# A second block group in the down projection, the gate's result in its operand's tile, and three smaller edits

## Chip, cores, metric

The kernel runs on one core of a Trainium2 chip. The metric is the device time of one execution in microseconds (us). Five engines work from queues of their own, each in order: PE (TensorE, matrix products), DVE (VectorE), ACT (ScalarE), POOL (GpSimd) and SP (SyncE, which here only issues transfers). An engine that waits at the head of its queue holds up everything queued behind it.

## What is computed

Two layers of a hybrid trunk over T = 1040 positions (16 learned meta tokens and 1024 frames), width 1024. Each layer: norm, one input projection, gated linear attention (GLA) in four heads beside softmax attention with a forget gate (FoX) in eight, an output projection, and a gated feed-forward network with 22 tiles of 128 hidden units.

```python
for i in range(DEPTH):
    xn = rms_norm(h, attn_norm[i])
    gq, gk, gv, gr, glr, fq, fk, fv, ff = jnp.split(xn @ w_in[i], cuts, axis=-1)
    ...
    o_gla = rms_norm(o_gla, ...) * jax.nn.silu(gr)
    ...
    h = h + jnp.concatenate([o_gla, o_fox], axis=-1) @ w_out[i]
    h = h + conv_ffn(rms_norm(h, ffn_norm[i]), w_up[i], conv_w[i], conv_b[i], w_down[i])
return rms_norm(h, final_norm)[:, N_META:]
```

The last step of `conv_ffn` is `(silu(g) * u) @ w_down`: 22 x 128 gated activations times a matrix with 1024 output columns. This is the down projection, where most of the change lies.

## The kernel before

**Products.** Values are kept transposed: 128 features on the partitions, positions along the row. Every fp32 operand is split into a rounded part `hi` (ACT casts) and a remainder `lo` (DVE subtracts), and `mm3` (L221 to L223) makes each product of three matmuls: hi*hi, lo*hi, hi*lo. Layer 0 works on all 1040 positions in two halves of 520 (two pieces of 260 columns each), layer 1 on 1024 in two halves of 512. PE's program is written out by hand; the order on DVE, ACT, POOL and SP is set by a scheduler from the program's dependences. Buffers of one row of T floats come from a shared pool of slots (`s.get`, `s.put`): a slot handed on makes its new writer wait until the old reader is done, be it an engine or a transfer.

**The down projection** (`ffn_down`) adds the products of 19 of the 22 gated tiles to the residual, in groups given by `GROUPS` (L49), each as kind, first tile, number of tiles. The last three tiles (`LAST`) are done by `down_last`, fused with the next layer's norm or with the output.

- "n", tiles 0 to 2: for each of 8 output tiles m, the plain product into PSUM; ACT copies it to a row `do` (L1510), and a transfer on POOL's queue adds the row to the residual `hm` in DRAM (L1512).
- "s", tiles 3 to 10, the block group (`down_blocks`): activations and weights are taken as 2 x 2 blocks (two halves of the hidden tiles; two output tiles, 2j and 2j+1; two halves of the positions), and 7 products of sums of blocks stand for 8. For each pair j the products 1 to 7 are formed in PSUM banks: `a` (two banks taken in turn by j; products 1, 6, 7 and 4 run on into the same sum), `y` for product 2, `x` for 5 and 3. After 1, 6, 7 and 4 ACT copies the sum out into row `du` or `dg` (L1423); after 2, 7 and 3 DVE adds the other bank's content (L1422). Finished rows go to `hm` by an adding transfer (L1437 for 2j+1, L1441 for 2j). The products' order is (0,1) (0,2) (1,1) (0,6) (0,5) (0,7) (0,4) (0,3), then for each later j (j,2) (j,6) (j,5) (j,7) (j+1,1) (j,4) (j,3). Sums of weight blocks are made by DVE (L1038) and split (L1055, L1056), up to four products ahead.
- "r", tiles 11 to 14 and 15 to 18: the residual rows `h0` to `h7` are loaded from `hm` into slots, and DVE adds each plain product to them (L1508).

The operands of later groups are prepared meanwhile (`prepare`, advanced by `pump`): the activations come from DRAM into `st` rows and are split into `ah`, `al` (L335, L336) or into block sums `x1` to `x7`. The weights of `LAST` (`wl`) are split in `down_last`.

**The gate.** `gr_products` (L601 to L631) multiplies a GLA head's output `gog` by silu of the gate, in three column tiles a head: DVE clips the gate into `ge` (L621), ACT takes exp, log and exp (L622 to L624), DVE forms the product in four steps (L625 to L629), the last into `ge` again, and a transfer on POOL's queue carries `ge` to `mixd` (L631). `ge` has one buffer, `gog` two, filled by a load.

**The end.** In the last layer `down_last` goes over three column chunks (512, 384, 128). Each product is added to `h` (L1586), squares are summed for the norm, and `final` scales the rows and stores them (`ot`, L1626). The final of chunk 0 is placed after m = 5 of chunk 1; that of chunk 1 after chunk 2.

**The first norm.** The sums of squares of the input are added on POOL, except those of its second chunk (`j == 1`), which are added on DVE.

## Time and profile before

| | |
|---|---|
| time, median of 3 runs | 2559.34 us (2559.17 to 2566.59) |
| profiled execution: time, span | 2563.32 us, 2561.5 us |
| mean granted TensorE clock | 0.992 |
| busy share of the span: PE, DVE, ACT, POOL | 98%, 69%, 50%, 16% |
| layer 0 down projection: "n", "s", both "r", `down_last` | 34.7, 83.8, 92.0, 34.2 us |
| layer 1: the same | 33.5, 81.2, 88.8, 40.4 us |
| from there to the end | 15.1 us |

The profile gives busy time by engine and by group of instructions, waits by releaser (the instruction or transfer whose end let an engine go on), and a timeline. A wait counted for PE is time in which PE stood; waits on the other engines cost only where PE waits for them later. PE's matmuls overlap: a 260-column one is listed with some 0.28 us, but the next one starts 0.12 us after it.

### The profile page before, as it was taken

The numbers are of one execution on the slowest core, as the hardware profiler recorded it, in microseconds if no ns is written. First come the engines' busy times: TensorE is split into PE (matmuls) and PEld (weight loads), VectorE is DVE, ScalarE is ACT, GpSimd is POOL, SyncE is SP. The second block draws the span as 40 slices with busy tenths as digits, with TensorE's granted clock in tenths as the row PEclk, the third lists the DMA queues.
The fourth block names the chain that finished last, engine by engine and source line by source line (L and its number), as shares of the span: only waits on it lengthen the run. The fifth ranks groups of instructions, "written<-read, shape, count | busy, mean of one in ns | idle before, by whom it ended". The sixth has DMA issues, their size and how long they took to land.

```text
span 2561.5 us, 47017 instructions
## 1 busy us (share of the span) xinstructions
PE 2502.1 (98%) x18430; PEld 2394.3 (93%) x18430; DVE 1776.7 (69%) x3493; ACT 1280.6 (50%) x2737; POOL 420.2 (16%) x587
## 2 busy tenths in 40 slices
PE   8999999999999999999999999999999999999997
PEld 7999999898999999999999899998999999997786
DVE  7656776859877777853666666677697777787545
ACT  6346666635544445641343466665464444455312
POOL 2023334310000000100200334333100000001003
PEclk9999999999999999999999999999999999999998
DMA  3132134342322223763312222143523222257711
GB/s 125 63 94 68 44 94 128 115 140 83 104 84 79 80 83 127 203 159 115 104 57 67 73 79 76 58 143 102 156 78 107 75 81 82 79 167 183 197 54 66
DMA packets 118510, 260.81 MB, mean 102 GB/s; under 512 B 14880, under 2 KB 32544, under 8 KB 118288
## 3 DMA queue, kind: packets, MB, share of 16 engines
q1 hardware_dynamic: 93984, 182.79, 22.9%
q0 software_dynamic: 22432, 72.71, 10.2%
q8 instruction: 144, 2.36, 0.4%
q10 hardware_dynamic: 1872, 2.31, 0.3%
q14 instruction: 78, 0.64, 0.1%
HBM read 177.16 MB, written 67.81 MB: 96 GB/s over the span
## 4 chain that ended last, share of the span: by engine, by line
PE 63%; issue 16%; DVE 12%; ACT 4%; DMA 3%; POOL 1%; SPq 0%; DVEq 0%; POOLq 0%; ACTq 0%
PE mm L221 7%; PE mm L223 7%; PE mm L222 7%; PE up L223 5%; PE up L221 5%; PE up L222 5%; PE down L221 5%; PE down L222 5%; PE down L223 5%; PE av L720 3%; PE tr L694 2%; DVE S L661 2%; ACT P L673 1%; PE S L658 1%; DVE x L1080 1%
## 5 line engine op out<-in xcount | busy, mean ns | idle before, releaser
L221 PE MATMUL up<-x,hi 128*128 128x260 f32 (+1 forms) x2464 | 698.1, 283 | 2.3 <-ACT x L1079 2.1
L223 PE MATMUL up<-x,hi 128*128 128x260 f32 (+1 forms) x2464 | 696.9, 283 | 3.1 <-DVE x L1080 2.9
L222 PE MATMUL up<-x,lo 128*128 128x260 f32 (+1 forms) x2464 | 696.8, 283 | 0.0
L223 PEld LDWEIGHTS up<-x,hi 128*128 128x128 f32 x2464 | 466.2, 189 | 4.6 <-DVE x L1080 4.6
L221 PEld LDWEIGHTS up<-x,hi 128*128 128x128 f32 x2464 | 465.1, 189 | 3.8 <-ACT x L1079 3.3
L222 PEld LDWEIGHTS up<-x,lo 128*128 128x128 f32 x2464 | 465.5, 189 | 0.4 <-DVE lo L1056 0.3
L1056 DVE TENSOR_TENSOR lo<-raw,hi 128x512 fp32r<-128x512 f32 x364 | 247.8, 685 | 176.2 <-ACT hi L1055 176.2
L221 PE MATMUL mm<-xh,hi 128*128 128x348 f32 (+4 forms) x1056 | 364.1, 345 | 0.0
L223 PE MATMUL mm<-xl,hi 128*128 128x348 f32 (+4 forms) x1056 | 340.0, 322 | 0.0
L222 PE MATMUL mm<-xh,lo 128*128 128x348 f32 (+4 forms) x1056 | 339.3, 321 | 0.0
L1055 ACT CAST hi<-raw 128x512 fp32r<-128x512 f32 x364 | 224.7, 620 | 136.9 <-PE up L223 91.3
L221 PEld LDWEIGHTS mm<-xh,hi 128*128 128x128 f32 x1056 | 199.9, 189 | 5.9 <-issue 5.3
L222 PEld LDWEIGHTS mm<-xh,lo 128*128 128x128 f32 x1056 | 199.8, 189 | 0.4 <-issue 0.3
L223 PEld LDWEIGHTS mm<-xl,hi 128*128 128x128 f32 x1056 | 198.8, 188 | 0.4 <-issue 0.3
L188 ACT CAST hi<-raw 128x512 fp32r<-128x512 f32 (+2 forms) x176 | 102.3, 582 | 190.4 <-PE down L223 106.6
L222 PE MATMUL down<-ah,lo 128*128 128x260 f32 (+1 forms) x528 | 169.2, 320 | 0.1
L221 PE MATMUL down<-ah,hi 128*128 128x260 f32 (+1 forms) x528 | 168.6, 319 | 0.0
L223 PE MATMUL down<-al,hi 128*128 128x260 f32 (+1 forms) x528 | 168.4, 319 | 0.0
L673 ACT ACTIVATE P<-S,m 116x460 f32<-116x460 f32 (+2 forms) x224 | 124.9, 561 | 78.4 <-DVE m L661 74.8
L336 DVE TENSOR_TENSOR PT<-tr,PT 116x464 fp32r<-116x464 f32 (+3 forms) x240 | 123.2, 515 | 48.0 <-ACT PT L335 46.1
L1268 POOL DMA_DIRECT2D actd<-cv x44 | 23.6, 536 | 761.0 <-DVE cv L1267 740.1
L1038 DVE TENSOR_TENSOR raw<-raw,raw 128x512 f32<-128x512 f32 x198 | 129.4, 683 | 15.4 <-DMA raw<-in_wd_dram 13.4
(286 smaller groups left out, 5680.9 us busy)
## 6 DMA issues: line engine op xcount, KB each, us to landing
raw<-in_wm_dram SPq DMA_DIRECT2D x330, 256.0 KB, 2.7
raw<-in_wd_dram SPq DMA_DIRECT2D x64, 256.0 KB, 3.6
actd<-cv POOLq DMA_DIRECT2D x22, 520.0 KB, 3.0
actd<-cv POOLq DMA_DIRECT2D x22, 512.0 KB, 3.2
cb<-cd SPq DMA_DIRECT2D x16, 520.0 KB, 3.8
st<-actd SPq DMA_DIRECT2D x14, 520.0 KB, 5.1
st<-actd SPq DMA_DIRECT2D x14, 512.0 KB, 4.8
kA<-kA SPq DMA_DIRECT2D x24, 260.0 KB, 4.3
```

The costliest lines, as they stand in the source:

```text
L188: nc.scalar.copy(hi[:, :n, :], raw[:, :n, :])
L221: nc.tensor.matmul(ps, wh, xh[:, c0:c0 + n], start=first, stop=False, skip_group_check=more)
L222: nc.tensor.matmul(ps, wl, xh[:, c0:c0 + n], start=False, stop=False, skip_group_check=more)
L223: nc.tensor.matmul(ps, wh, xl[:, c0:c0 + n], start=False, stop=last, skip_group_check=more)
L336: nc.vector.tensor_tensor(out=lo, in0=src, in1=hi.bitcast(F32), op=ALU.subtract)
L661: nc.vector.tensor_tensor_reduce(out=S[:rows, :n], in0=S[:rows, :n], in1=cb[:rows, c0:k1], scale=1.0, scalar=(BIG if ci == 0 else m[:rows, ...
L673: nc.scalar.activation(P[:rows, :n], S[:rows, :n], AF.Exp, scale=-1.0, bias=m[:rows, nch - 1:nch], accum_out=(den if nch == 1 else d3[:row ...
L694: nc.tensor.transpose(tr[:w, 3 - j, :rows], P[:rows, o:o + w], id_)
L720: nc.tensor.matmul(av[:, a:b], w.rearrange("p a b -> p (a b)"), x, start=(t == ts[0] and part == 0 and i == 0), stop=(t == last and i == 1))
L1038: nc.vector.tensor_tensor(out=q[out][:, :nk, :], in0=q[a][:, :nk, :], in1=q[b][:, :nk, :], op=op)
L1055: nc.scalar.copy(hi[:, :nk, :], src[:, :nk, :])
L1056: nc.vector.tensor_tensor(out=lo[:, :nk, :], in0=src[:, :nk, :], in1=hi[:, :nk, :].bitcast(F32), op=ALU.subtract)
```

## The change

1. `GROUPS` becomes n(0,3), s(3,8), n(11,4), s(15,4). Tiles 11 to 14 go through ACT copies and adding transfers, tiles 15 to 18 through a second block group with two hidden tiles in each half (the first has four), so that each of its 28 products is half as long. The residual is loaded late: `h7` and `h6` when product (2,7) of that group is issued, the others as slots come free. For its last pair (output tiles 6 and 7) DVE adds the finished row to `h6`, `h7` in place of the transfer.
2. The weights of `LAST`: the first two tiles are prepared during the second block group.
3. The gate's last step writes into `gog` instead of `ge`, and the transfer to `mixd` reads `gog`.
4. The first norm's second chunk: POOL adds the squares of even k, DVE those of odd k.
5. The end: the final of chunk 0 is placed after m = 3 of chunk 1, and that of chunk 1 is held until the last product has been added to `h`.

```diff
-GROUPS, LAST = (("n", 0, 3), ("s", 3, 8), ("r", 11, 4), ("r", 15, 4)), (19, 3)
+GROUPS, LAST = (("n", 0, 3), ("s", 3, 8), ("n", 11, 4), ("s", 15, 4)), (19, 3)
...
-            to = e if dst is None else dst[:, c0:c0 + n]
+            to = og if dst is None else dst[:, c0:c0 + n]
...
-                nc.gpsimd.dma_start(self.mixd[h][:, c0:c0 + n], e)
+                nc.gpsimd.dma_start(self.mixd[h][:, c0:c0 + n], og)
...
+        def out(j, m, t):
+            if residual and j == NP - 1:
+                h = residual(m)[:, o0:T]
+                nc.vector.tensor_tensor(out=h, in0=t[:, o0:T], in1=h, op=ALU.add)
+            else:
+                nc.gpsimd.dma_start(self.hm[m][:, o0:T], t[:, o0:T], accum_op=ALU.add)
+            s.put(t)
...
+                if residual and (j, p) == (NP - 2, 7):
+                    residual(KD - 1), residual(KD - 2)
...
+        def residual(k):
+            if hT[k] is None:
+                hT[k] = s.get(F32, f"h{k}", first=ids)
                 nc.sync.dma_start(hT[k][:, o0:T], self.hm[k][:, o0:T])
+            return hT[k]
...
-                    blocks = self.down_blocks(lyr, *nxt, X[nxt[0]], pp, fw, halves,
-                                              lambda t=then: len(ahead) < 2 and fetch(t))
+                    more = (lambda t=then: len(ahead) < 2 and fetch(t)) if then else \
+                        (lambda: len(self.last_w[0]) < 2 and self.last_weight(lyr, ids))
+                    blocks = self.down_blocks(lyr, *nxt, X[nxt[0]], pp, fw, halves, more, None if then else residual)
...
-            if not hT:
-                load_residual()
+            for k in range(KD):
+                residual(k)
...
-                elif m == 5 and c0 != dchunks[0][0]:
+                elif m == (5 if c0 + n == T else 3) and c0 != dchunks[0][0]:
                     self.norm_scale(nxt, pp, *before)
...
-                self.final(nxt, hT, pp, *before, pool=KD + 1)
+                with self.tc.issue_after(summed.ins):
+                    self.final(nxt, hT, pp, *before, pool=KD + 1)
...
-                    "square": lambda j: [self.norm_square(nm, *part(j, k), nc.vector if j == 1 else None) for k in range(KD)],
+                    "square": lambda j: [self.norm_square(nm, *part(j, k), nc.vector if j == 1 and k % 2 else None) for k in range(KD)],
```

Line numbers below are those of the changed kernel where its rows are shown: L336 and L337 are the casts and remainders of activations (L335, L336 before), L1056 and L1057 those of weight blocks, L1039 the sums of weight blocks, L1522 and L1524 the "n" copies and their transfers, L1432 and L1433 the block group's adds and copies.

**DVE in the gate, layer 0, at 441 to 445 us of the profile before.** `S`, `m` are a FoX head's scores and row maxima, `PT` its transposed probabilities, `fa`, `fv`, `fy`, `fd` small values of its norm, `gx` the gate's value. Before:

```order
L743 TENSOR_REDUCE fv<-fon 112x2
L625 TENSOR_TENSOR gog<-gx,gog 128x348
L744 TENSOR_TENSOR fv<-fv,fd 112x2
L661 ISA S,m<-S,cb 116x460
L661 ISA m 116x1
L278 SCALAR_TENSOR_TENSOR fa<-fy 112x2
L741 SCALAR_TENSOR_TENSOR fd<-den 116x4
L621 TENSOR_SCALAR ge<-gx 128x348
L279 TENSOR_TENSOR fa<-fa,fv 112x2
L661 ISA S,m<-S,cb,m 116x348
```

Now:

```order
L744 TENSOR_REDUCE fv<-fon 112x2
L622 TENSOR_SCALAR ge<-gx 128x348
L745 TENSOR_TENSOR fv<-fv,fd 112x2
L626 TENSOR_TENSOR gog<-gx,gog 128x348
L662 ISA S,m<-S,cb 116x460
L662 ISA m 116x1
L742 SCALAR_TENSOR_TENSOR fd<-den 116x4
L662 ISA S,m<-S,cb,m 116x348
```

The clip into `ge` has moved ahead of the first of the two score steps; it no longer waits for a transfer that reads `ge`.

**ACT where tiles 11 to 14 end and the second block group begins, layer 0.** Before, the place between the two "r" groups held nothing but weight casts:

```order
L188 CAST hi_14768<-raw_14766 128x512
L188 CAST hi_14826<-raw_14824 128x512
L188 CAST hi_14884<-raw_14882 128x512
L188 CAST hi_14942<-raw_14940 128x512
L188 CAST hi_15000<-raw_14998 128x512
```

Now (`down_14913` and `down_14939` are the two halves of m = 7; `ah_15375` is the last tile's activation, in the slot that row `do_14458` of m = 6 had):

```order
L1056 CAST hi_14901<-raw_14893 128x256
L1522 COPY do_14459<-down_14913 128x520
L336 CAST ah_15375<-st_15179 128x1040
L1522 COPY do_14459<-down_14939 128x520
L1056 CAST hi_14966<-raw2_14905 128x256
L1433 COPY du_14983<-down_14970 128x520
L1056 CAST hi_15004<-raw2_14828 128x256
```

The cast of `ah_15375` stands between the two copies of m = 7. It cannot run before the adding transfer of m = 6 has read its row.

**DVE at the same place, now** (`du_14983`, `dg_15078` are the rows of j = 0; `down_15045` is bank `x`; `al_15376` takes the slot that row `do_14459` of m = 7 had):

```order
L1432 TENSOR_TENSOR du_14983<-down_14990,du_14983 128x520
L1057 TENSOR_TENSOR lo_15025<-raw_14830,hi_15024 128x256
L1039 TENSOR_TENSOR raw2_15204<-raw2_15120,raw2_15122 128x256
L337 TENSOR_TENSOR al_15376<-st_15179,ah_15375 128x1040
L1057 TENSOR_TENSOR lo_15042<-raw_14899,hi_15041 128x256
L1039 TENSOR_TENSOR raw2_15120<-raw_15118,raw2_15120 128x256
L1039 TENSOR_TENSOR raw_14899<-raw_14899,raw2_15060 128x256
L1057 TENSOR_TENSOR lo_15063<-raw2_15060,hi_15062 128x256
L1039 TENSOR_TENSOR raw2_15206<-raw2_15204,raw_15118 128x256
L1057 TENSOR_TENSOR lo_15082<-raw2_15058,hi_15081 128x256
L1432 TENSOR_TENSOR dg_15078<-down_15045,dg_15078 128x520
```

The remainder `al_15376` now stands ahead of six builds and of the add that frees bank `x` after (0,7); it waits for the transfer of m = 7. Before, DVE had one add for each half product here (L1508) and the remainders of weights.

More of the change, by code (lines that the diff above doesn't have):

```diff
@@ L1436, in evacuate @@
                 copy(q["g"][:, t0])
[L1437 to L1438 removed]
+                out(j, 2 * j + 1, q["g"])
             elif p == 3:
                 add(q["u"][:, t1], q["x"])
[L1441 to L1442 removed]
+                out(j, 2 * j, q["u"])
                 del st[j]
@@ L1477, in ffn_down @@
         two = lambda ap: ap.rearrange("p (a b) -> p a b", b=n)
-        hT, ahead, going = [], [], []
-        def load_residual():
-            for k in range(KD):
-                hT.append(s.get(F32, f"h{k}", first=ids))
+        hT, ahead, going = [None] * KD, [], []
+        def residual(k):
+            if hT[k] is None:
+                hT[k] = s.get(F32, f"h{k}", first=ids)
                 nc.sync.dma_start(hT[k][:, o0:T], self.hm[k][:, o0:T])
+            return hT[k]
         def complete(done):
@@ L1494, in plain @@
                 complete(lambda: all(j in acts for j in range(g0, g0 + ng)))
-                if kind == "r" and not hT:
-                    load_residual()
+                if kind == "r":
+                    for k in range(KD):
+                        residual(k)
             if kind == "n" and m == 0:
@@ L1555, in run @@
                 ahead.clear()
-            if not hT:
-                load_residual()
+            for k in range(KD):
+                residual(k)
             complete(lambda: all(j in acts for j in range(LAST[0], sum(LAST))))
@@ L1566, in ffn_down, with last_weight @@
         return tail, run
+    def last_weight(self, lyr, es):
+        w, held = self.last_w
+        m, (g0, ng) = len(w), LAST
+        if m % 2 == 0:
+            held += [self.slots.get(F32R, "wl", (128, 2, 4, 128), es) for _ in range(2)]
+        w.append(self.weights(self.wd[lyr, m][:, g0:g0 + ng, :], [x[:, m % 2, :, :] for x in held[-2:]]))
     def down_last(self, lyr, hT, pp, dchunks, acts, at_end, es):
@@ L1571, in down_last @@
         g0, ng = LAST
-        w, held = [], []
-        for m in range(KD):
-            if m % 2 == 0:
-                pair = [s.get(F32R, "wl", (128, 2, 4, 128), es) for _ in range(2)]
-                held += pair
-            w.append(self.weights(self.wd[lyr, m][:, g0:g0 + ng, :], [x[:, m % 2, :, :] for x in pair]))
+        while len(self.last_w[0]) < KD:
+            self.last_weight(lyr, es)
+        (w, held), self.last_w = self.last_w, ([], [])
         nxt = at_end()
@@ L1585, in down_last @@
                 h = hT[m][:, c0:c0 + n]
-                nc.vector.tensor_tensor(out=h, in0=ps[:, :n], in1=h, op=ALU.add)
+                summed = nc.vector.tensor_tensor(out=h, in0=ps[:, :n], in1=h, op=ALU.add)
                 final = nxt["gain"] is None
```

7 lines of the change are left out of this document (2 added, 5 removed).

## The prediction, made before the changed kernel ran

> **What bounds the kernel now.** I read the page's head first, then PE's waits over the whole span (line of the waiting operation, releaser: us in total, times, longest).
>
> ```profile
> span 2561.5 us, 47017 instructions
> PE 2502.1 (98%) x18430; PEld 2394.3 (93%) x18430; DVE 1776.7 (69%) x3493; ACT 1280.6 (50%) x2737; POOL 420.2 (16%) x587
> ...
> PE S L658 <- ACT P L673: 6.6, 9, 1.9
> ...
> PE down L221 <- ACT dg L1423: 2.7, 4, 0.7
> PE down L221 <- ACT du L1423: 2.1, 2, 1.1
> ...
> PE mm L221 <- DVE h L1586: 1.2, 1, 1.2
> ...
> PE mm L222 <- DVE wl L190: 0.4, 1, 0.4
> ```
>
> PE is busy 98% of the span, so only two things can shorten it: fewer matmuls, or fewer of these waits. No other engine is near its limit over the whole. The stages that the change rewrites are next: time, PE busy, PE's instructions, then the same for the weight loads, DVE, ACT and POOL, the clock, the DMA share.
>
> ```profile
> 1071.20:1155.00 83.80, 81.34 (x675) 80.71 (x674) 42.35 (x56) 34.23 (x53) 6.83 (x8) 1.00 0.65 176
> 1155.00:1247.00 92.00, 92.00 (x770) 92.00 (x769) 37.48 (x57) 13.95 (x24) 0.85 (x1) 1.00 0.34 97
> 1247.00:1281.20 34.20, 34.20 (x218) 34.20 (x218) 25.93 (x43) 19.42 (x41) 16.71 (x16) 1.00 0.34 122
> 2336.00:2417.20 81.20, 78.81 (x339) 62.91 (x338) 43.34 (x58) 33.97 (x53) 6.90 (x8) 1.00 0.65 176
> 2417.20:2506.00 88.80, 88.80 (x385) 72.02 (x384) 36.16 (x55) 13.13 (x22) 0.86 (x1) 1.00 0.32 94
> ```
>
> Rows two and five are the "r" groups: PE never stands, one matmul each 92.00/770 = 0.1195 us (260 columns) and 88.80/385 = 0.2306 us (512). Row three is `down_last` of layer 0. Rows one and four are the block group: the same rate, but PE stands 2.4 us in each. The block group needs fewer matmuls and loses some of the gain at hand-overs.
>
> **1. The second block group: what it saves.** 7 products for 8 over four tiles: 384 matmuls become 336 in layer 0, 192 become 168 in layer 1. 48 x 0.1195 + 24 x 0.2306 = 5.7 + 5.5 = 11.3 us.
>
> **2. Its hand-overs.** PE at the two sharp places of the first block group:
>
> ```profile
> 1088.44 0.28 PE L223 MATMUL down<-x,hi 128*128 128x260 f32 x1
> 1089.41 0.39 PE L221 MATMUL down<-x,hi 128*128 128x260 f32 x1 [0.68 <-ACT dg L1423]
> ...
> 1145.33 0.39 PE L221 MATMUL down<-x,hi 128*128 128x260 f32 x1 [1.10 <-ACT du L1423]
> ...
> 1149.15 0.39 PE L221 MATMUL down<-x,hi 128*128 128x260 f32 x1 [0.68 <-ACT dg L1423]
> ```
>
> (0,4) and (3,4) follow (0,7) and (3,7) in the same bank with no product between, so PE waits for the copy: 1089.41 - 1088.44 is 0.97 against 0.12, and the restart is some 0.1 slower, 0.95 us. The new group has both places: 4 x 0.95 = 3.8 us over two layers. Everywhere else at least one product lies between, now of 12 matmuls, 1.43 us, where it was 2.87. That still covers 0.95 if ACT is at most 0.48 late, about one build; I take 0.5 us a layer for the times when it is not (a `wl` cast stands before a copy there, and waits for the adding transfer of (0,4)'s row), 0 to 3: 1.0 us in all.
>
> At the end of the first block group the 1.10 above goes. It is caused here (ACT):
>
> ```profile
> 1143.72 1.06 ACT L335 CAST ah<-st 128x1040 fp32r<-128x1040 f32 x1 [0.38 <-DMA st<-actd]
> 1144.69 0.59 ACT L1423 COPY du<-down 128x520 f32<-128x520 f32 x1
> ```
>
> Two `ah` casts for the "r" group come before the copy; now block sums do, with loads that come earlier. But one such cast also stands before the copy of (3,7), which I price at 0.6 to 0.8 us a layer. Net gain 2.1 - 1.4 = 0.7 us.
>
> **3. Its entry, the largest unknown.** The row shown above for ACT puts `ah` between the copies of m = 7, behind the adding transfer of m = 6; DVE has `al` behind that of m = 7. Nothing like it stands before the first block group, whose PE goes on without a wait. Their landing is what counts (from issue; "n" rows, then block rows):
>
> ```profile
> L1512 POOL DMA_DIRECT2D hm<-do x16: 853/862/891, 1042.1 to 2337.4; - x16
> ...
> DMA to landing us min/median/max: 5.2/5.9/9.2
> ```
>
> ```profile
> L1437 POOL DMA_DIRECT2D hm<-dg x8: 853/859/862, 1093.5 to 2415.4; - x8
> ...
> DMA to landing us min/median/max: 5.3/5.5/8.8
> ```
>
> And the pieces that follow a landing:
>
> ```profile
> 1070.80 1.07 ACT L335 CAST ah<-st 128x1040 fp32r<-128x1040 f32 x1 [0.84 <-PE down L223]
> 1071.77 0.58 ACT L1510 COPY do<-down 128x520 f32<-128x520 f32 x1
> ```
>
> ```profile
> 1071.90 1.24 DVE L336 TENSOR_TENSOR al<-st,ah 128x1040 fp32r<-128x1040 f32 x1
> ...
> 1089.79 0.69 DVE L1422 TENSOR_TENSOR dg<-down,dg 128x520 f32<-128x520 f32 x1
> ...
> 1275.06 0.42 DVE L1586 TENSOR_TENSOR h<-mm,h 128x256 f32<-128x256 f32 x1
> ```
>
> Count from the end of m = 7 on PE. m = 6 ends 48 x 0.1195 = 5.74 us earlier; its copy is done and its transfer issued at -4.8. At 5.6 us to landing that is +0.8. The cast (1.07) and the copy (0.58) end at about +2.5, and that copy frees the bank of (0,2), which could begin at +1.43: 1.15 us lost. The transfer of m = 7 then goes out at +2.6 and lands near +8.7, if it takes 6.1, since the load of `h6` runs beside it. `al` (1.24), six builds of about 0.42 and the add (0.69) end at +13.2; (0,3), which needs that bank, could begin at +12.2: 0.95 lost with the start of the add. Together 2.1 us a layer, 4.2 in all. Bounds: with landings at the row's minimum 5.2 and the casts early, 0.3 a layer; with both near the maximum, 8.8, it is 4.35 and 3.6, 8.0 a layer.
>
> [...] The trace has no adding transfer under 5.2 us, and I go by it.
>
> Down projection: 11.3 - 3.8 - 1.0 + 0.7 - 4.2 = 3.0 us gained. The late loads of `h0` to `h5` and six `wl` splits stand before DVE's first adds in `down_last`. I cost them at nothing: a matmul there takes 34.20/218 = 0.157 us, an output tile 9 of them, so PE fills six PSUM banks in 8.5 us before it needs one back. Without that cover the loss is DVE's backlog, six splits of the `wl` size and what a late `h0` adds, 2 to 5 us. With the first `wl` ahead, the 0.4 us wait on `wl` goes.
>
> **4. The gate.** DVE and PE in both layers, then what DVE waited for before `ge` over the whole run:
>
> ```profile
> 444.73 0.34 DVE L621 TENSOR_SCALAR ge<-gx 128x348 f32<-128x348 f32 x1 [1.69 <-DMA mixd<-ge]
> ...
> 446.89 0.47 PE L658 MATMUL S<-kA,qA 128*116 128x460 f32 x1 [1.75 <-ACT P L673]
> ```
>
> ```profile
> 1627.52 0.34 DVE L621 TENSOR_SCALAR ge<-gx 128x348 f32<-128x348 f32 x1 [1.79 <-DMA mixd<-ge]
> ...
> 1629.68 0.50 PE L658 MATMUL S<-kA,qA 128*116 128x460 f32 x1 [1.91 <-ACT P L673]
> ```
>
> ```profile
> DMA mixd<-ge: 3.8, 4
> ```
>
> The transfer still reads `ge` when the next tile wants it; DVE stands, then ACT's exp of `ge` and of the scores behind it, then PE. With the result in `gog` this wait has no cause, and PE's 1.75 + 1.91 go. I take 3.5 us of the 3.7, 1.0 to 3.9: what comes late next may be the exp itself. The new wait is on `gog`: a tile's load waits for the transfer of the tile two before it, not one.
>
> **5. The end.** DVE's six scalings of chunk 0 hold up the adds that PE needs:
>
> ```profile
> 2538.14 6.74 DVE L1626 SCALAR_TENSOR_TENSOR ot<-h,vec,r 128x512 f32<-128x512 f32 x6
> 2544.81 0.67 DVE L1586 TENSOR_TENSOR h<-mm,h 128x128 f32<-128x128 f32 x3
> ...
> 2552.33 0.28 DVE L1586 TENSOR_TENSOR h<-mm,h 128x128 f32<-128x128 f32 x1
> 2552.53 1.67 DVE L1626 SCALAR_TENSOR_TENSOR ot<-h,vec,r 128x384 f32<-128x384 f32 x3
> ```
>
> Two output tiles earlier is about 3 us earlier, so the first adds of chunk 2 are no longer behind all six, and PE's 1.2 us wait on `h` goes; the last add also stands ahead of the scalings of chunk 1. The scalings after it are the same work. 1.7 us, 0 to 3.
>
> **6. The head.** POOL takes three sums of squares from DVE; PE's row there is
>
> ```profile
> 40.15 0.48 PE L387 MATMUL mm<-xl,both 128*64 128x256 f32 x1 [1.53 <-DVE xl L297]
> ```
>
> DVE comes to `xl` a little earlier, but the norm's factor then waits for POOL: 0.3 us, -1 to 1.
>
> **Sum.** 3.0 + 0.4 + 3.5 + 1.7 + 0.3 = 8.9 us. The profiled execution took 2563.32 (span 2561.5 and 1.8 around it) and would take 2554.4; it lies 4.0 above the median of the runs. Against 2559.34 that is 2550.4, which I round to 2550.5.
>
> **The rivals.**
>
> *Late landings (slower).* If the transfers of m = 6 and m = 7 land later than the 5.6 and 6.1 us above, each us costs PE one us at (0,2) and, as the second transfer then also goes out later, one more at (0,3): 2 a layer, 4 in all. The gain is gone at 8.9/4 = 2.2 us more, about 8 us; beyond that the kernel is slower than before. At 8.8 for both the entry costs 16.0 in place of 4.2: 2550.5 + 11.8 = 2562.3. For it: the last "n" transfer in both layers took that long, with loads beside it, and such loads are beside these. Against it: 5.9 is the median, and the loads here are half as large. [...]
>
> *Nothing late.* Landings at 5.2, casts early, no loss between products: 8.9 + 3.6 + 1.0 = 13.5 us, 2545.8. For it: ACT and DVE are half idle. Against it: the queues are in order, and idle time before a landing helps nobody.
>
> *The gate's wait only moves.* If the load of `gog`, which now waits for the transfer, is as late as `ge` was, the 3.5 us stay: 2554. For it: the same transfer's landing is in the chain, with a load of its own behind it. Against it: two buffers in place of one.
>
> **How the numbers follow.** My forecast 45%, late landings 22%, nothing late 18%, the gate's wait moving 15%. 0.3%, about what the measurement tells from no change, is 7.7 us: faster is below 2551.7, slower above 2567.0. The forecast's own spread is 2547 to 2554, two thirds of it below 2551.7: 30%. With all of "nothing late" that is 48% faster. Late landings spread from 2556 to 2572, as other adding transfers (fourteen more in each layer) may be late with them: 12% slower, 10% within. With the gate's 15% and the forecast's other 15%, 40% within. The range is 2541 to 2566: below, "nothing late" with the upper bounds of the end (1.3 more) and of the hand-overs and the head (some 3 more); above, landings of 9.2 for both (2550.5 + 4 x 3.35 = 2563.9) and two us lost elsewhere. What is worse than that is left to the remaining 2 in 10.
>
> **What would show it.** Stage times of the second pair of groups: 92.0 us in layer 0 should become about 90.0 to 91, 88.8 in layer 1 about 87.5. PE's waits should list `dg` L1433 with eight sharp places in place of four, and new ones on ACT `do` and DVE `dg` at the entry, near 1.2 and 1 us. No wait on `mixd` before `ge`, PE's wait of 1.8 and 1.9 on `P` gone. In the last stage no wait on `h`. It is wrong if the entry's waits are over 4 us a layer, if DVE waits for `gog`, or if `down_last` stands for `h0`.

## The result, and the profile after

| | before | changed |
|---|---|---|
| median of 9 runs each | 2560.08 us (2557.14 to 2566.59) | 2570.39 us (2567.62 to 2575.75) |
| ratio, 95% interval | | 1.0035 [1.0025, 1.0046] |
| profiled execution: time, span | 2563.32, 2561.5 us | 2567.62, 2565.9 us |

The kernel became slower by about 10 us, 20 us away from the forecast and outside its range. The changed kernel's profiled execution is the shortest of its nine.

The head of its page, then PE's waits over the whole span (releaser: us in total, times, longest):

```profile
span 2565.9 us, 47155 instructions
PE 2491.2 (97%) x18358; PEld 2383.5 (93%) x18358; DVE 1790.6 (70%) x3540; ACT 1327.0 (52%) x2847; POOL 449.3 (18%) x618
...
PE down L222 <- ACT dg L1433: 14.3, 10, 3.0
...
PE down L222 <- ACT do L1522: 5.1, 2, 2.6
...
PE mm L222 <- ACT wl L189: 3.4, 1, 3.4
...
PE ssq L322 <- POOL r L311: 2.8, 1, 2.8
...
PE S L659 <- ACT P L674: 2.2, 4, 0.7
...
PE mm L222 <- DVE h L1604: 1.1, 2, 0.7
```

PE has 72 matmuls less and is busy 10.9 us less. But `dg`, 2.7 us before, is 14.3 now, `do` and the first `wl` are new, and the last stage has a wait on POOL. The wait on `P` fell from 6.6 to 2.2, as the gate's edit wanted. The stages, in the columns shown before ("s" (3,8), "n" (11,4), "s" (15,4), `down_last` in layer 0, the first three in layer 1):

```profile
1063.90:1148.90 85.00, 81.18 (x675) 80.55 (x674) 48.22 (x64) 34.46 (x54) 6.83 (x8) 1.00 0.63 158
1148.90:1194.90 46.00, 46.00 (x387) 46.00 (x386) 12.25 (x21) 15.21 (x28) 6.82 (x8) 1.00 0.76 144
1194.90:1244.90 50.00, 42.98 (x339) 41.94 (x338) 22.59 (x47) 20.17 (x45) 5.97 (x7) 0.97 0.69 157
1244.90:1281.20 36.30, 35.11 (x219) 34.23 (x218) 26.94 (x45) 18.94 (x40) 14.86 (x14) 1.00 0.58 202
2336.40:2418.70 82.30, 78.60 (x337) 62.82 (x336) 49.07 (x66) 34.13 (x54) 6.90 (x8) 1.00 0.64 163
2418.70:2463.00 44.30, 44.30 (x193) 36.04 (x193) 12.27 (x21) 15.02 (x28) 6.91 (x8) 1.00 0.76 146
2463.00:2510.40 47.40, 40.64 (x170) 31.12 (x169) 22.32 (x47) 19.98 (x45) 6.04 (x7) 1.00 0.71 161
```

The second pair of groups takes 46.00 + 50.00 = 96.0 us for 92.0, and 44.3 + 47.4 = 91.7 for 88.8. In the new block group PE stands 7.0 and 6.8 us. At the rates of before it would need 336 x 0.1195 = 40.2 and 168 x 0.2306 = 38.7 us. The first block group and `down_last` have become longer too, though their products are the same.

Three places show how. First, the end of the first block group in layer 0 (ACT, then PE):

```profile
1139.17 1.07 ACT L336 CAST x<-t 128x1040 fp32r<-128x1040 f32 x1 [1.45 <-DVE t L1362]
1140.49 2.02 ACT L336 CAST x<-st 128x1040 fp32r<-128x1040 f32 x2 [0.25 <-DVE st L1362]
1142.42 0.58 ACT L1433 COPY dg<-down 128x520 f32<-128x520 f32 x1
...
1143.06 0.39 PE L222 MATMUL down<-x,hi 128*128 128x260 f32 x1 [2.67 <-ACT dg L1433]
```

Three casts of block sums for the later group stand in ACT's queue ahead of the copy that frees the bank; the first two wait for sums that DVE has not made yet. PE waits 2.67 us, 2.69 in layer 1. Second, the entry of the new block group (POOL, ACT, PE):

```profile
1190.26 0.85 POOL L1524 DMA_DIRECT2D hm<-do  x1 [4.89 <-ACT do L1522]
...
1197.39 1.06 ACT L336 CAST ah<-st 128x1040 fp32r<-128x1040 f32 x1 [4.57 <-DMA hm<-do]
1198.36 0.58 ACT L1522 COPY do<-down 128x520 f32<-128x520 f32 x1
...
1198.99 0.39 PE L222 MATMUL down<-x,hi 128*128 128x260 f32 x1 [2.53 <-ACT do L1522]
```

The slot that `ah` wants belongs to the row whose adding transfer was issued at 1190.26; it is handed on at 1197.39, 7.1 us later (6.9 in layer 1: 2458.63 to 2465.57). Third, the first weights of `LAST` inside that group:

```profile
1220.84 0.51 ACT L189 CAST wl<-raw 128x384 fp32r<-128x384 f32 x1 [4.34 <-DMA raw<-in_wd_dram]
1221.26 0.58 ACT L1433 COPY dg<-down 128x520 f32<-128x520 f32 x1
...
1221.89 0.39 PE L222 MATMUL down<-x,hi 128*128 128x260 f32 x1 [2.98 <-ACT dg L1433]
```

ACT stands 4.34 us for a load, with the copy that PE needs right behind. All three are one mechanism, with 1.45, 4.57 and 4.34 us of ACT in the rows above: an instruction that nobody needs yet waits at the head of an in-order queue, ahead of a copy that PE does need. In the pair of "r" groups that stood here before, DVE alone took PE's results and ACT copied nothing, so such casts held up no one (PE was busy 92.00 of 92.00 us).

### The profile page after: what moved, and what is told of

Its sections match the earlier page's. It is cut to its first block, busy times and chain, and to the rows that moved or that the text cites. A ratio compares the mean times of both kernels' runs of the same rounds, so it can differ in the third digit from the quotient of the medians.

```text
span 2565.9 us, 47155 instructions
## 1 busy us (share of the span) xinstructions
PE 2491.2 (97%) x18358; PEld 2383.5 (93%) x18358; DVE 1790.6 (70%) x3540; ACT 1327.0 (52%) x2847; POOL 449.3 (18%) x618
## 4 chain that ended last, share of the span: by engine, by line
PE 78%; DVE 12%; ACT 4%; DMA 3%; issue 2%; POOL 0%; DVEq 0%; SPq 0%; POOLq 0%; ACTq 0%
PE up L222 11%; PE up L223 11%; PE up L224 11%; PE mm L222 7%; PE mm L223 7%; PE mm L224 7%; PE down L222 4%; PE down L223 4%; PE down L224 4%; PE av L721 3%; PE tr L695 2%; DVE S L662 2%; PE S L659 1%; ACT P L674 1%; PE S L660 1%
## 5 line engine op out<-in xcount | busy, mean ns | idle before, releaser
L1057 DVE TENSOR_TENSOR lo<-raw,hi 128x512 fp32r<-128x512 f32 (+1 forms) x420 | 270.8, 650 | 225.1 <-ACT hi L1056 224.9
L1056 ACT CAST hi<-raw 128x512 fp32r<-128x512 f32 (+1 forms) x420 | 246.8, 592 | 154.8 <-PE up L224 93.4
L222 PE MATMUL down<-x,hi 128*128 128x260 f32 (+1 forms) x504 | 163.5, 324 | 21.3 <-ACT dg L1433 14.3
L1039 DVE TENSOR_TENSOR raw<-raw,raw 128x512 f32<-128x512 f32 (+1 forms) x230 | 142.2, 647 | 42.3 <-DMA raw<-in_wd_dram 38.1
L223 PE MATMUL down<-x,lo 128*128 128x260 f32 (+1 forms) x504 | 161.9, 321 | 0.0
L224 PE MATMUL down<-x,hi 128*128 128x260 f32 (+1 forms) x504 | 161.6, 321 | 0.0
L337 DVE TENSOR_TENSOR PT<-tr,PT 116x464 fp32r<-116x464 f32 (+3 forms) x240 | 122.6, 514 | 47.2 <-ACT PT L336 45.4
L189 ACT CAST hi<-raw 128x512 fp32r<-128x512 f32 (+2 forms) x160 | 92.5, 579 | 83.9 <-PE wo L224 38.9
```

The lines of the kernel that those rows point to most:

```text
L189: nc.scalar.copy(hi[:, :n, :], raw[:, :n, :])
L222: nc.tensor.matmul(ps, wh, xh[:, c0:c0 + n], start=first, stop=False, skip_group_check=more)
L223: nc.tensor.matmul(ps, wl, xh[:, c0:c0 + n], start=False, stop=False, skip_group_check=more)
L224: nc.tensor.matmul(ps, wh, xl[:, c0:c0 + n], start=False, stop=last, skip_group_check=more)
L337: nc.vector.tensor_tensor(out=lo, in0=src, in1=hi.bitcast(F32), op=ALU.subtract)
L1039: nc.vector.tensor_tensor(out=q[out][:, :nk, :], in0=q[a][:, :nk, :], in1=q[b][:, :nk, :], op=op)
```

## The experiments

In every comparison the kernel before ran on the same chip; its median there was 2560.4 to 2562.0 us. Stage times are from the profiled execution, from a stage's first matmul to that of the next.

**1. Everything but the groups.** The kernel before with the gate's edit, the head's and the end's.

> The kernel before with three of the five edits (gate result in its operand's tile, first norm's sums on two engines, other order at the end) and the groups as they were. Stages by PE's first matmul. If the gain in the attention stages of the changed kernel comes from the gate edit (theory): layer 0's up-projection starts near 584.5 us (590.3 before), the waits of 1.7 us before the clip into the gate tile are gone in both layers, PE's waits on the probabilities fall from 6.6 to about 2.2 us, and the whole is 8 to 11 us faster than before, near 2550. Rival (that gain was an accident of one execution, or came from the new groups): start near 590, whole within 3 us of 2560. At the end of the kernel: last stage to the end 55.5 us if the new order there gives nothing, 53.8 if it gives the 1.7 us of the prediction.

Measured: 2551.48 us against 2561.22, ratio 0.9964 [0.9952, 0.9975]. As the theory had it: the small edits gain, so the groups must lose nearly 20. At the end of the kernel nothing came: from the last stage's first product to the end it takes 55.6 us, 55.5 before.

**2. The gate alone.** The kernel before with

```diff
-            to = e if dst is None else dst[:, c0:c0 + n]
+            to = og if dst is None else dst[:, c0:c0 + n]
...
-                nc.gpsimd.dma_start(self.mixd[h][:, c0:c0 + n], e)
+                nc.gpsimd.dma_start(self.mixd[h][:, c0:c0 + n], og)
```

> The kernel before with the gate edit alone. The three edits without the groups gave 9.7 us; the traces put some 2.7 of that before 46 us (the first norm), nothing at the end, the rest in the two attention stages. If so: 6 to 7 us faster than before, near 2554, layer 0's up-projection 4 to 5 us earlier than 590.3, and layer 1's attention as much shorter. If the gate gives only the two waits named in the prediction (3.5 us): near 2557.5, and the rest of the 9.7 is the first norm's or an accident.

Measured: 2552.42 us against 2561.57, ratio 0.9963 [0.9949, 0.9976], a gain of 9.2, more than either expectation. The gate alone gives what the three small edits give together. PE's wait on `P`:

```profile
PE S L658 <- ACT P L673: 2.2, 4, 0.7
```

That is 4.4 us less than before. DVE's waits show more of it. Besides the 3.8 us on `mixd` it stood before the gate's product (`gy` is ACT's last exp):

```profile
DVE ge L626 <- ACT gy L624: 6.3, 8, 0.8
```

With the edit:

```profile
DVE ge L626 <- ACT gy L624: 1.2, 2, 0.6
```

In the same two attention stages PE had short waits on `P` and `PT`, and most of them went too (last section). The 2.7 us before 46 us came here as well, although the first norm is unchanged: the kernel before runs at half clock (granted clock 0.50) from 39.4 to 46.2 us of its profiled execution, this one does not.

**3. The groups alone.** The changed kernel with the gate, the head and the end as before.

> The changed kernel with the gate, the first norm's sums and the end as they were before: the second block group, the late residual and the last weights ahead alone. If the two halves of the change simply add (theory): 2561.2 + (2570.4 - 2551.5) = about 2580, second pair of groups 96 and 91.6 us as in the changed kernel, layer 0's up-projection near 590 us. Rival (they interact: the other edits make room that the groups use, or the reverse): more than 4 us off 2580.

Measured: 2579.31 us against 2560.39, ratio 1.0069 [1.0053, 1.0086], +18.9. With the -9.7 of the first experiment that makes +9.2, close to the change's own +10.3: the two parts add up.

**4. Activation splits behind the copies.** In the second block group, the preparation of `LAST`'s activations (`pump`) is held until the copy of the current step has been issued:

```diff
-            copy = lambda out: nc.scalar.copy(two(out), q["a"][:, :pieces, :n])
+            copy = lambda out: marks.__setitem__(0, nc.scalar.copy(two(out), q["a"][:, :pieces, :n]).ins)
...
-                    self.pump(1, 3)
+                    if residual:
+                        with self.tc.issue_after(marks[0]):
+                            self.pump(1, 3)
+                    else:
+                        self.pump(1, 3)
```

> The changed kernel; only the split of the last tile's activation is held behind the block group's last copy, so that it no longer stands between the two copies of m = 7. Theory (a head of queue that waits for a transfer): PE's wait on the copy of m = 7 (2.5 and 2.6 us) goes in both layers and so does the 0.7 us on the add; second pair of groups 96.0 to about 93.2 us in layer 0, 91.6 to 88.2 in layer 1; whole about 6 us faster than the changed kernel, near 2564. Rival (the short products leave ACT and DVE too little time, the wait only moves to the next hand-over): both stages within 1 us of 96.0 and 91.6, whole near 2570. Rival (transfers late by contention): as the theory for the wait itself, but others grow by as much.

Measured: 2564.28 us, ratio 1.0014 [1.0005, 1.0024], 6.1 under the changed kernel's median. PE's list has no wait on `do` left; the new block group takes 45.9 and 44.3 us in place of 50.0 and 47.4. The waits on `dg` did not grow for it (13.4 us in all, 14.3 in the changed kernel). The entry is shown.

**5. First weights behind the copies.** The same hold on the first two tiles' weights of `LAST`:

```diff
-                        after()
+                        if residual:
+                            with self.tc.issue_after(marks[0]):
+                                after()
+                        else:
+                            after()
```

> The changed kernel; only the casts of the last tiles' first weights are held behind the block group's latest copy, so that none stands ahead of the copy after product (1,7). Theory (the cast waits at the head of ACT's queue for its slot, which an adding transfer of product (0,4)'s row still reads, and for its own load): PE's waits there of 3.0 us in layer 0 and 1.9 in layer 1 go; second pair 96.0 to 93.0 and 91.6 to 89.8 us; whole 4.5 to 5 us faster, near 2565.5. Rival (too little time between products): the same 3 us appear at another copy, stages unchanged, near 2570. If the last weights are then late, the stage after it begins with a wait on them, up to 2 us.

Measured: 2565.89 us, ratio 1.0015 [1.0005, 1.0024], 4.5 under the changed kernel. The block group takes 46.7 and 43.8 us, PE's waits on `dg` are 9.4 in place of 14.3.

**6. Block sums behind the copies.** The hold on the casts for the later group, during the first block group and the first step of "n" (11,4):

```diff
...
+                        self.copied = marks[0]
+                        with self.tc.issue_after(marks[0]):
+                            self.pump(1, 3)
...
-                self.pump(2)
+                if kind == "n" and g0 == 11 and m == 0:
+                    with self.tc.issue_after(self.copied):
+                        self.pump(2)
+                else:
+                    self.pump(2)
```

> The changed kernel; only the casts of the second group's block sums are held behind the first block group's latest copy, so that at most those of sums 1 and 2 stand ahead of the copy after its product (3,7). Theory (that copy waits behind casts whose own operands DVE has not made yet): PE's wait of 2.7 us at the end of the first block group falls to the 0.7 us of the copy in both layers; first block group 85.0 to about 83 us and 82.4 to 80.5; whole 4 us faster than the changed kernel, near 2566.5. Rival (the casts are late there because the slots' transfers are late, and only move): the same 2 us appear at the start of the plain group behind it, which is at 46.0 and 44.3 us without a wait now; whole near 2570.

Measured: 2562.33 us, ratio 1.0009 [0.9999, 1.0019], 8.1 under the changed kernel, more than expected. The first block group, layers 0 and 1:

```profile
1062.40:1144.70 82.30, 80.94 (x674) 80.51 (x673) 43.95 (x58) 31.47 (x51) 6.83 (x8) 1.00 0.64 159
2330.90:2410.60 79.70, 78.35 (x337) 62.92 (x336) 45.46 (x61) 31.24 (x51) 6.90 (x8) 1.00 0.67 167
```

82.3 and 79.7 us, below the 83.8 and 81.2 before: the waits on `du` in this stage, made by casts of the same kind (1.10 and 1.03 us before, 0.48 and 0.34 in the changed kernel), go too. The two stages show 5.3 of the 8.1 us. The likely rest is the half clock that was seen behind 34 of 45 waits of 2.2 to 3.4 us (last section); this is not shown for it alone.

**7. Order of the residual's loads** in the last stage:

```diff
-            for k in range(KD):
+            for k in (4, 5, 0, 1, 2, 3, 6, 7):
```

> The changed kernel; only the order in which the residual rows ask for slots after the second block group is another: 4, 5, 0, 1, 2, 3 in place of 0 to 5, so that rows 0 and 1, finished first and used first, get the slots that come free first. Theory (DVE's adds at the start of the fused last stage are late because row 0 is loaded after that stage has begun, and with them ACT's and DVE's feed of the next layer): layer 0's last stage 36.3 to about 34.5 us, and the wait of 3.4 us on the weights that follows (with 0.6 more) falls under 1; whole 5 us faster, near 2565. Rival (DVE's backlog is the weights' splits, not the loads): last stage above 35.8, the wait on the weights stays over 2 us, whole near 2570.

Measured: 2568.51 us, ratio 1.0032 [1.0019, 1.0044]. `down_last` of layer 0 is back at 34.5 us for 36.3, and its wait on `h` is gone, as expected. The order is not the only thing that moves this stage: without it the stage took 34.3 us in experiments 3 and 6, 34.9 in 4 and 37.0 in 5. The wait for the first weights of the next input projection (also called `wl`) stayed at 3.4: a miss on that half, and the time is not distinguishable from the changed kernel's.

**8. Weight remainders on POOL**, with that order: the subtractions of `LAST`'s later weights go from DVE to POOL.

```diff
-            eng = nc.gpsimd if self.att else nc.vector
+            eng = nc.gpsimd if self.att or self.on_pool else nc.vector
...
+        self.on_pool = m >= 2
```

> The changed kernel with the order of the residual rows of the run before, and the remainders of the last six output tiles' weights made on POOL, not on DVE. Theory (what is left of the backlog after the last stage, PE's wait of 3.4 us on the next layer's first weights, is DVE's: six splits of 0.55 us each stand among its adds, ACT's feed and cast wait for these): the wait falls under 1.5 us, whole 3 us faster than with the order alone, near 2565. Rival (the wait is on the slot of those weights, read by the last product of the stage, or on their place in ACT's queue): it stays at 3 us or over, whole 2568 to 2570.

Measured: 2571.09 us, ratio 1.0047 [1.0032, 1.0061]. The wait stayed at 3.4, so these remainders on DVE are not its cause. ACT there:

```profile
1252.93 0.51 ACT L190 CAST wl<-raw 128x384 fp32r<-128x384 f32 x1 [4.41 <-DMA raw<-in_wd_dram]
1253.35 0.63 ACT L298 ACTIVATE xh<-h,vec 128x400 fp32r<-128x400 f32 x1
```

The cast waits for a load, with the first `xh` of the next layer behind it. In the changed kernel, and in the one before:

```profile
1253.69 0.51 ACT L189 CAST wl<-raw 128x384 fp32r<-128x384 f32 x1 [5.46 <-DMA raw<-in_wd_dram]
1254.11 0.63 ACT L297 ACTIVATE xh<-h,vec 128x400 fp32r<-128x400 f32 x1
```

```profile
1249.51 0.63 ACT L296 ACTIVATE xh<-h,vec 128x400 fp32r<-128x400 f32 x1 [2.75 <-DVE h L1586]
```

The first `xh` begins 9.3 us after the stage's start at 1244.86 where it was 2.4 us after 1247.07. The first cast of the input projection's weights stands behind 22 of the 24 `xh` in both kernels; it begins 42.1 us after the stage's start where it was 36.3, so ACT does not catch up.

**9. The last pair of weights behind the first feed.** The casts of `LAST`'s tiles for the last pair of outputs are issued after output tile 2 has been squared for the norm, and no longer ahead of the stage's products; with the order of 7.

> The changed kernel with the other order of the residual rows; the weights of the last two output tiles are cast behind the feed of output tile 2 in place of ahead of the first feed. Theory (ACT stands 4.4 us at the cast of these weights, whose load waits for a buffer and for the residual's loads; the first feed stands behind it, and the chain of add, feed and remainder runs at PE's pace and never makes it good): PE's wait of 3.4 us on the next layer's first weights falls below 1 us, the whole 3 to 4 us below the run with the order alone, near 2565. Rival (those weights wait for their slot, read by the stage's last product): the wait stays at 3 us, near 2568.5.

Measured: 2568.93 us, ratio 1.0027 [1.0016, 1.0038]. PE's row:

```profile
PE mm L222 <- ACT wl L189: 1.4, 1, 1.4
```

3.4 became 1.4, which supports the reading of 8, but the total is not distinguishable from the changed kernel's. A miss on the time.

**10. All holds together:** 4, 5, 6, 7 and 8 in one kernel.

> The changed kernel with all of these together: last tile's split, last weights' first casts and block sums behind the copies, residual rows in the other order, remainders on POOL. Theory (each wait had a cause of its own): second pair 46.0 + 42.6 and 44.3 + 42.4 us, first block group 83 and 80.5, whole 2570.4 - 6 - 4.5 - 4 - 4 = about 2552 if the wait on the next layer's weights stays, 2549 if it goes; that is beside the kernel with the other three edits alone (2551.5). Rival (the short products are too tight): the gains overlap and the whole stays above 2557.

Measured: 2548.20 us against 2560.39, ratio 0.9955 [0.9942, 0.9968]: 22 us under the changed kernel and 12 under the one before. PE's waits, then the stages of the two block groups, "n" and `down_last`:

```profile
PE down L222 <- ACT dg L1433: 5.4, 8, 0.7
...
PE mm L223 <- ACT wl L190: 2.7, 1, 2.7
```

```profile
1061.20:1143.50 82.30, 80.94 (x673) 80.51 (x673) 43.75 (x58) 31.48 (x51) 6.83 (x8) 1.00 0.65 159
1143.50:1189.50 46.00, 46.00 (x387) 46.00 (x386) 15.77 (x25) 17.88 (x31) 6.84 (x8) 1.00 0.74 144
1189.50:1232.40 42.90, 40.86 (x338) 40.23 (x337) 22.39 (x47) 20.18 (x45) 6.08 (x8) 1.00 0.87 200
1232.40:1266.70 34.30, 34.30 (x219) 34.30 (x218) 24.77 (x40) 20.15 (x42) 23.27 (x20) 1.00 0.57 197
```

Eight sharp hand-overs of 0.7 us are left, the ones that the prediction counted, and PE stands 2.0 us in the new block group where it stood 7.0.

**11. The same with the last pair behind the feed** (9 in 10, without the remainders on POOL).

> All moves together (last tile's split, first of the last weights, block sums, order of the residual rows) with the last pair of weights behind the feed in place of the remainders on POOL. Theory: as the run with all moves, less its wait of 2.7 us on the next layer's weights: 2548.2 - 3 = about 2545; layer 0's down projection with its last stage 237 us (244.7 before), 240 in the run with all moves. Rival (PE then waits for the last pair's weights in the stage itself): 2548 or more.

Measured: 2548.36 us, ratio 0.9944 [0.9932, 0.9957]. The rival came: the wait moved into `down_last`, which takes 40.1 us, with PE waiting 3.0 for the late pair. No gain over 10.

**12. Only the three holds** (4, 5, 6).

> Only the three holds that paid alone: the later casts of the second block group, the first weights of LAST and the block sums around the first block group each stand behind the copy of their step. The residual's order and the weight remainders are as in the changed kernel. If the three do not overlap, the gains of 6, 4.5 and 8 us add up: 2570.4 - 18.5 = about 2552, and if the other two edits of the joint kernel cost a little (2571.1 against 2570.4 for the remainders on POOL, with the residual's order), 2546 to 2549: then their place is better left alone. PE's waits: dg on ACT under 6 us in all, none on do; the stage s(15,4) 42 to 43.5 us in layer 0 and 42 in layer 1; the wait on the first weights of layer 1 near 3.4 as in the changed kernel. Rival: the residual's order or the remainders on POOL carried part of the joint gain, through the last stage (34.3 us there in the joint kernel): then the last stage stays at 35 to 37 us and the time is 2551 or more.

Measured: 2551.23 us against 2561.99, ratio 0.9965 [0.9951, 0.9978]. The three gains of 6.1, 4.5 and 8.1 add up to 18.7, and 19.2 is what came. The rest of experiment 10, about 3 us by the medians though the intervals overlap, lies in the last stage (37.4 us here, 34.3 there), as the rival said. Whether the residual's order or the remainders carry it stays open: the order alone brought that stage to 34.5, but experiments 3 and 6 had 34.3 with neither.

## Why the prediction was wrong, step by step

**What it saves (11.3 us): right.** The matmuls are gone and the rate held: the "n" group takes 384 x 0.1198 us, and with the holds in place the new block group takes 42.9 and 41.9 us, the bare 40.2 and 38.7 plus some 3.

**The sharp places (-3.8): right in size.** The rows of experiment 10 show eight of 0.7 for the four that were there.

**The end of the first block group (+0.7): wrong.** The prediction called block sums harmless since their loads come earlier, and let one cast delay the copy of (3,7) by 0.6 to 0.8. But their operands are sums that DVE makes, late, and three casts stood there. PE lost 2.67 and 2.69 us in place of the 0.7 of a sharp place and the 0.6 to 0.8 of the cast, and of the waits on `du` that were to go 0.48 and 0.34 stayed. Holding these casts back gained 8.1 us (experiment 6).

**Between products (-1.0): wrong, the largest miss of the new group itself.** The step saw a `wl` cast ahead of a copy, with a transfer that it waits for, but priced it by ACT's own delay, up to one build. The cast waited for its load, 4.34 us in layer 0, though ACT was busy for only 20.17 of the stage's 50.0 us: that made 2.98 and 1.88 us of PE, over the step's upper bound of 3, and 4.5 of the time (experiment 5).

**The entry (-4.2): mechanism right, size off.** (0,2) waits on `do` behind an `ah` cast, as described, but the transfer of m = 6 released the slot after 7.1 and 6.9 us, not 5.6, so 1.15 became 2.53 and 2.58. The 0.95 at (0,3) came in layer 1 alone, as 0.69. In all 5.8 us of waits for 4.2, and the hold that removes them gained 6.1 (experiment 4). The rival "late landings" thus came, some 1.4 us late where it needed 2.2, and its second us at (0,3) did not: a later landing cost about 2 us for each us, not 4. Alone it would have taken some 2 us off the gain. One reading there is too wide: 5.2 us is the shortest of the adding transfers into `hm`; ten adding loads of weights (L1032, 256 KB each) landed in 3.9 to 5.0.

**`down_last` (0) and the first weights (+0.4): wrong.** The cover named, six PSUM banks, held for the first 33 us of `down_last` and then failed: PE stood 0.70 and 0.44 us for DVE's adds to `h`. What came late was the feed of the next layer behind ACT's weight casts. PE lost 2 us in `down_last` and 3.4 + 0.6 at the next weights. The prediction looked at DVE's queue and not at ACT's. Moving DVE's remainders away did not help (experiment 8), moving ACT's casts took the wait from 3.4 to 1.4 (experiment 9). No kernel here with the new group is rid of it without a loss elsewhere.

**The gate (3.5): right and too small.** The wait on `mixd` and PE's two waits behind it are gone; it gave 9.2. The sum had only these two. It left out DVE's 6.3 us on `gy`, PE's short waits beside them, and the half clock behind the longer of the two (last section). The rival that its wait only moves is refuted (experiment 2).

**The end (1.7): wrong.** Experiments 1 and 2 gain 9.7 and 9.2 us, a difference within their intervals for the end and the head together, and from the last stage's first product to the end the profile has 55.5 us before and 55.5 now. The wait on `h` went and another came: DVE's six scalings still hold four adds behind them, and POOL's share of the sums of squares is late with them.

```profile
2539.32 6.74 DVE L1645 SCALAR_TENSOR_TENSOR ot<-h,vec,r 128x512 f32<-128x512 f32 x6
2545.99 1.40 DVE L1604 TENSOR_TENSOR h<-mm,h 128x384 f32<-128x384 f32 x4
...
2549.41 1.65 PE L322 MATMUL ssq<-r,ones 128*128 128x384 f32 x2 [2.81 <-POOL r L311]
```

**The head (0.3): nothing to see.** PE is 2.7 us ahead of the kernel before at 57 us in experiment 1 and as much in experiment 2, which has the old head.

**What no step had: the clock behind a wait.** See the last section. In the sum, the down projection and the weights behind it, +3.4 forecast, came out at -15.4 in the profiled execution (7.5 and 4.3 us longer in the two layers from the first "n" to the end of `down_last` and of the second block group, and 3.4 + 0.6 at the weights for 0.4); the gate gave back 5.7 more than forecast, and the 2.0 of the end and the head did not come. That makes some 15 of the 19 us between the forecast gain of 8.9 and the measured loss of 10.3. The rest is of the size of the clock's part; since one execution and medians are mixed here, it can't be said closer.

Of the three signs of being wrong that the prediction named none came: the entry cost 2.5 and 3.3 us a layer, DVE did not wait for `gog`, and PE did not stand for `h0` (DVE did, 1.7 us at the start of `down_last`). The losses lay in places that it had priced at little or nothing.

## What to carry to other kernels

Where a scheduler fills an in-order queue, ask of every instruction that may come ahead of a copy which frees a PSUM bank what it waits for: if it is a slot that a transfer still reads, a load, or another engine's sum, its price is the whole of that wait (here 4.34 us), not its own duration (0.51). Moving work onto an engine that had no deadline (ACT's casts between two "r" groups) gives every instruction already queued there a deadline; here PE's waits on ACT's `dg` went from 2.7 to 14.3 us. Hold such work behind the copy, and test the holds together: each alone left the changed kernel no faster than before; all of them made it faster by 12 us, of which the gate alone gives 9. The block group is then worth some 3 us over the small edits alone (2548.20 against 2551.48), with intervals that overlap. That is near the 3.4 forecast for it, but by luck: the forecast was for a kernel without the holds, and that one lost.

## What the hardware showed

**In the down projection and at the weights behind it the granted clock was 0.50 for 3.4 us or more after 34 of 45 waits of PE of 2.2 to 3.4 us, and the place of a wait on a grid of 3.413 us sorts them.** In each of the 14 profiles (before, changed and twelve experiments) the granted clock is either 1.00 or 0.50. The stretches at 0.50 last 3.413 us or a multiple up to the last, which runs to the end, and they start whole multiples of 3.413 us apart, to within 5 ns, on a grid that lies differently against the program in each execution. At 0.50 matmuls of 260 columns start 0.216 us apart, at 1.00 0.120 (changed kernel, from 1199.97 us); 3.41 x (1 - 0.120/0.216) makes some 1.5 us lost in a stretch of 3.41, an estimate. Six windows of that grid in the changed kernel, in pairs (PE busy is the second number, the clock follows POOL's):

```profile
1196.56:1199.97 3.41, 0.98 (x8) 0.98 (x9) 0.42 (x1) 2.58 (x5) 0.74 (x1) 1.00 0.43 131
1199.97:1203.39 3.42, 3.42 (x19) 3.42 (x18) 1.88 (x4) 0.48 (x2) 0.12 (x1) 0.50 0.80 160
...
1217.04:1220.45 3.41, 1.88 (x16) 1.67 (x14) 0.37 (x1) 0.00 (x0) 0.00 (x0) 1.00 0.82 183
1220.45:1223.87 3.42, 1.98 (x16) 1.98 (x17) 1.46 (x3) 2.34 (x6) 0.00 (x0) 1.00 0.00 0
...
1285.33:1288.74 3.41, 0.47 (x2) 0.21 (x2) 2.94 (x7) 3.18 (x8) 1.97 (x3) 1.00 0.23 79
1288.74:1292.15 3.41, 3.41 (x10) 3.41 (x11) 3.41 (x6) 2.35 (x6) 3.10 (x4) 0.50 0.58 167
```

The 2.53 us at the entry fall almost whole into one window, in which PE is busy for 0.98 us, and the next window runs at half clock. The longer wait of 2.98 behind `wl` is cut by a boundary of the grid into 1.54 and 1.44, and no such window follows. Of the 3.39 at the first weights 2.33 lie in one window, and one follows.

In the down projection and at the first weights behind it, over all 14 profiles, this sorts all 61 waits of over 1.0 us: the 35 with 1.86 us or more in one window were followed by half clock, for 3.4 us (6.8 in five cases); the 26 with 1.82 or less were not. By length alone it looks like chance: 34 of 45 waits of 2.2 to 3.4 us were followed, one of 16 between 1.0 and 2.2, and none of 111 between 0.6 and 1.0 that do not stand right behind a longer one. Elsewhere in the program the limit is less sharp: of 36 windows in which PE stood 1.5 to 1.86 us 25 were followed. The 1.91 us wait on `P` in the kernel before lies whole in one window and was followed:

```profile
1630.00:1632.00 2.00, 2.00 (x11) 1.88 (x9) 1.93 (x5) 1.39 (x6) 0.00 (x0) 0.50 0.00 0
```

The half clock also moves single profiles. Outside the last 28 us, where PE has little to do, it takes 6 times 3.41 us of the changed kernel's profiled execution and 13 times of that of experiment 7, at 1.5 us each some 10.5 us more; the spans differ by 10.3 (2565.9 and 2576.2), with a last stage of layer 0 that is 1.8 shorter. In the down projection and at the weights behind it the changed kernel has six waits of over 2.2 us, of which two were followed; at three in four it would be two or three more in another execution. That fits the median lying 2.8 us above the profiled one, and the granted clock of the other eight executions, 0.987 to 0.991 against 0.993.

The granted clock of every execution, averaged, gives an estimate of the clock's part. In experiment 3 it is 0.9908, against 0.9934 for the kernel before on the same chip: 0.0026 x 2577.7 us is 6.7, and with the 1.5 us above in place of half of each 3.41 some 5.9, of the 18.9 lost. With the three holds (experiment 12) it is 0.9934 against 0.9933, so that loss is gone with the waits. For the gate alone it is 0.9932 against 0.9929, about 1 us of its 9.2: most of that gain is PE's waits.

The profiled executions of the kernel before and of experiment 2, product by product, show where. They differ by 11.5 us. Of this 2.8 lie before 48 us, at the half clock from 39.4 to 46.2, where the gate has no part. The attention stages differ by 4.5 and 6.1 us: 4.4 are the waits on `P` as they are listed, some 1.5 the half clock behind the second long one (matmuls of 344 columns start 0.287 us apart there, 0.158 elsewhere). The rest lies in steps of 0.3 to 0.5 us at short waits on `P` and `PT`, which cost more than their length: the product `S` at 362.41 is listed with a wait of 0.25 and starts 0.57 us after the one ahead of it, where experiment 2 has 0.16. Against this, experiment 2 has one stretch at half clock at 1356 us that the kernel before has not. That DVE's waits on `gy` make these short waits is likely from their place, and not shown by a run of its own.
